# A second half of the feed-forward layer in a seven-product form, with weight sums made by accumulating DMAs

## The chip, the cores and the metric

The kernel runs on one core of one Trainium2 chip. The metric is the device time of one execution in microseconds (us); lower is better. The core has a matrix engine (PE, with weight loads listed as PEld), a vector engine (DVE), a scalar engine (ACT), GpSimd (POOL), and a synchronisation engine (SP) that issues most of the DMAs. PE adds its sums into PSUM; the other operands stand in SBUF, and the large arrays in DRAM.

## The reference

The reference is a decoder trunk of two layers on 1024 tokens of width 1024, in float32. Each layer has a mixer and then a feed-forward part, which is what the change touches:

```python
for layer in range(DEPTH):                       # DEPTH = 2
    ...
    x = x + y                                    # y: the mixer's output
    h = rmsnorm(x, ffn_norm_g[layer])
    x = x + jnp.square(jax.nn.relu(h @ ffn_w1[layer])) @ ffn_w2[layer]
return rmsnorm(x, final_norm_g)
```

`ffn_w1` is 1024 x 4096 and `ffn_w2` is 4096 x 1024. The product with `ffn_w2` is called the output product below, the one with `ffn_w1` the input product.

## The kernel before

All arrays are held transposed: features on the 128 partitions, the 1024 tokens along the free axis, so a tile of 128 x 1024 float32 (512 KB) is one block of features. `X` is eight such tiles. Every dense product is made in three terms. An operand is split into a high part (ACT casts it, line 99) and a low remainder (DVE subtracts, line 100), and a block of 128 x 128 weights meets a slice of activations in three matmuls: high by high, high by low, low by high (lines 149 to 151). In the names, `wr` is a weight tile as loaded, `wh` and `wl` are its parts; `ft` is a loaded tile of the hidden layer, `fh` and `fl` are its parts. There are 3 buffers for `wr` and 8 for `wh` and `wl` together, that is four weight tiles; the 128 x 1024 tiles of all other kinds (`ft`, `fh`, `fl`, `x`, `hid` and more) come from one pool of 34 slots.

`ffn` (line 430) does the feed-forward part. It first calls `ffn_in` (line 298), which makes the input product already in a seven-product form: each of 16 units makes two feature blocks of the hidden layer in seven products of a quarter of the size (names B11, B21, T2, T1, T3, B22, T4), with the sums `T2`, `T1`, ... of the activations and the sums `S1`, `S2`, ... of the weights made on DVE. The unit takes relu and square on ACT and stores the two tiles `hid` to DRAM by DMAs that ACT issues (lines 408 and 411).

The output product then goes in eight chunks over K (4096). `hload(c)` loads the four hidden tiles of a chunk, DVE multiplies each by `acc`, which by then holds the squared scale of the norm (line 443), and they are split. `out_chunk` (line 269) loads the weights of the chunk in four tiles, and for each of them makes two output blocks in two halves of 512 tokens: 12 matmuls (4 hidden tiles by three terms) into a PSUM tile `mm`, which DVE adds into `X` (line 293). In the last chunk the tokens go in four segments of 256 (`SEGS`), so that the norm of the next layer (`norm_sq`, `norm_fin`) can be made segment by segment beside it; after layer 1 that is the final norm, and `norm_fin` stores to the output.

A scheduler places the instructions of each engine in an order; each engine, SP too, then runs its own list in order, and an instruction that waits holds up all that stand behind it on the same engine. `high_priority(HP)` moves splits and evictions ahead in that order. DMAs issued by SP and ACT go through two queues (q1 and q10 of the page).

Of the kernel before, what the change touches and what calls it, by code (L numbers as in the profile page):

```python
# [35 lines left out]
def hs(half):  # L36
    return slice(half * HALF, (half + 1) * HALF)
# [7 lines left out]
def R(ap):  # L45
    return ap.bitcast(F32R)
# [10 lines left out]
class Trunk:  # L57
# [131 lines left out]

    def norm_start(self, X, g, split=True):  # L190
        lo = [self.slot("hl") for _ in range(NT)]
        hi = [self.slot("hh") for _ in range(NT)] if split else None
        return dict(X=X, g=g, acc=None, lo=lo, hi=hi, split=split)

    def norm_sq(self, st, i, r):
        nc = self.nc
        if st["acc"] is None:
            st["acc"] = self.slot("acc")
        if i == 0:
            nc.scalar.activation(st["acc"][:, r], st["X"][0][:, r], AF.Square)  # L200
        else:
            t = self.small([P, r.stop - r.start], "sq")
            self.sq = nc.scalar.activation(t, st["X"][i][:, r], AF.Square)
            nc.vector.tensor_tensor(st["acc"][:, r], st["acc"][:, r], t, ALU.add)

    def norm_fin(self, st, r, ps=None):
        nc, split = self.nc, st["split"]
        n = r.stop - r.start
        if ps is None:
            ps = self.psum_parts(st["acc"], r)  # L210
# [68 lines left out]
    def out_chunk(self, wsrc, acts, X, norm=None, fill=0, segs=(hs(0), hs(1))):  # L279
# [26 lines left out]
        else:  # L306
            ws = [[self.wload(src[ob]) for src in wsrc] for ob in range(4)]
            for j, r in enumerate(segs):
                for ob in (0, 2, 1, 3):
# [4 lines left out]
                    if not wino and j > 0 and ob == 2:  # L314
                        self.norm_fin(norm, segs[j - 1])


    def ffn_in(self, l, st, hid, load):

        nc, ops, tt = self.nc, st["ops"], self.nc.vector.tensor_tensor  # L320
# [61 lines left out]
        def square(t, src=None):  # L382
            self.last_relu = nc.scalar.activation(t, t if src is None else src, AF.Relu)
            nc.scalar.activation(t, t, AF.Square)

        def unit(u, ws):
# [24 lines left out]
            nc.scalar.dma_start(hid[2 * u + 1], h1)  # L411

# [17 lines left out]
    def ffn(self, l, st, xd, norm_g):  # L430
        nc = self.nc
        hid = self.dp.tile([FF // P, P, T], F32, name=self.nm("hid"))
        w2 = self.a["w2"][l]
        X = [self.slot("x") for _ in range(NT)]
        norm = norm_g(X)

        def hload(c):
            hs_ = []
            for k in range(4 * c, 4 * c + 4):
                t, hh, hl = self.slot("ft"), self.slot("fh"), self.slot("fl")  # L440
                nc.sync.dma_start(t, hid[k])
                with self.tc.high_priority(HP):
                    nc.vector.tensor_tensor(t, t, st["acc"], ALU.mult)
                    self.last_split = self.split(t, hh, hl)
                hs_.append((hh, hl))
            return hs_

        cur = self.ffn_in(l, st, hid, hload)
        with self.tc.issue_after(self.last_split.ins):
            for o in range(NT):  # L450
                nc.sync.dma_start(X[o], xd[o])
# [4 lines left out]
        return X, norm  # L456

# [416 lines left out]
    def conf_half(self, i, ws, half, acts, fill=0, nlow=0, fin=None):  # L874
# [5 lines left out]
        if fin is not None:  # L880
            self.norm_fin(fin, SEGS[-1])
        pg = self.mm_ps()
# [218 lines left out]
    def odd(self, st, norm_g):  # L1101
# [9 lines left out]
        prs = [self.conf_pair(i) for i in range(2)]  # L1111
        self.conf_half(0, prs[0], 0, acts, fin=st)
        self.conf_half(1, prs[1], 0, acts)
        for i in range(2):
            self.conf_half(i, prs[i], 1, acts)
            self.conv31(i, prs[i][2])
# [58 lines left out]
    def build(self):  # L1175
        tc, nc, a = self.tc, self.nc, self.a
        with tc.tile_pool(name="kp", bufs=1) as self.kp, tc.tile_pool(name="wp", bufs=1) as self.wp, \
# [18 lines left out]

            st = self.norm_start(X, "mixg0")
            self.gmlp(st)
            X, norm = self.ssd(st, lambda X: self.wino_start(X, "ffng0", self.xd[0]))
# [10 lines left out]
            X, norm = self.ffn(1, norm, self.xd[2], lambda X: self.norm_start(X, "fing", False))  # L1210
            self.norm_fin(norm, SEGS[-1])

def layout(inputs):
# [52 lines left out]
    r["w1"] = np.stack([blocks(f("ffn_w1")[l]) for l in range(2)])  # L1268
    r["w2"] = np.stack([kout(f("ffn_w2")[l], 4, 256) for l in range(2)])
    return r  # L1270
# [20 lines left out]
```

## Time and profile before

| | |
|---|---|
| time, median of 3 runs | 2853.62 us (2852.7 to 2854.3) |
| profiled execution: its own time | 2856.86 us |
| profiled execution: span, first to last instruction | 2855.1 us |
| PE busy | 2815.4 us (99%) |
| DVE / ACT / POOL busy | 1927.6 (68%) / 1198.3 (42%) / 4.0 us |
| DMA traffic | 287.23 MB, mean 101 GB/s |

The profile is of one execution, so its parts add up to its own time of 2856.86 us, which is 3.2 us above the median. A busy share is of the whole span; a wait that matters shows as a hole in PE's row.

### The profile page before, as it was taken

How to read it: one execution, taken by the hardware profiler on the slowest of the kernel's cores; microseconds unless marked ns; L12 is line 12 of the kernel's file. 1: busy time of each engine (PE TensorE's matmuls, PEld its weight loads, DVE VectorE, ACT ScalarE, POOL GpSimd, SP SyncE). 2: the span in 40 equal slices, each digit the busy share in tenths (PEclk: the TensorE clock that was granted, in tenths of full speed). 3: DMA queues.
4: the chain of work that ended last, by engine and by line, in shares of the span. 5: the costliest groups of instructions: out<-in, count | busy, mean ns of one | idle time of the engine just before them, and what ended most of it. 6: DMA issues, size and time to landing. Idle time of an engine off the chain costs nothing.

```text
span 2855.1 us, 36628 instructions
## 1 busy us (share of the span) xinstructions
PE 2815.4 (99%) x14637; PEld 2361.8 (83%) x14637; DVE 1927.6 (68%) x2985; ACT 1198.3 (42%) x1964; POOL 4.0 (0%) x16
## 2 busy tenths in 40 slices
PE   8999998999999999999999999998999999999998
PEld 8988786778788888889888888888888888888887
DVE  5666878768544566546699998885769544566546
ACT  6421425226655532113534444455347655522112
POOL 0000000000000000000000000000000000000000
PEclk9999999999999999999999999999999999999999
DMA  4131424513333453221211111113313332543211
GB/s 163 45 98 64 140 66 149 188 52 111 118 118 102 150 191 128 86 74 46 102 52 60 63 57 53 53 59 126 139 52 104 133 105 102 175 180 118 85 56 60
DMA packets 100027, 287.23 MB, mean 101 GB/s; under 512 B 10768, under 2 KB 33680, under 8 KB 99856
## 3 DMA queue, kind: packets, MB, share of 16 engines
q1 hardware_dynamic: 83440, 242.47, 26.0%
q10 hardware_dynamic: 16416, 42.42, 3.8%
q8 instruction: 115, 1.88, 0.3%
q14 instruction: 56, 0.46, 0.1%
HBM read 217.61 MB, written 67.24 MB: 100 GB/s over the span
## 4 chain that ended last, share of the span: by engine, by line
PE 93%; DVE 5%; ACT 1%; DMA 1%; issue 1%; SPq 0%; DVEq 0%
PE mm L149 19%; PE mm L151 19%; PE mm L150 19%; PE mm L330 6%; PE mm L331 6%; PE mm L332 6%; PE mm L160 3%; PE mm L161 3%; PE mm L162 3%; DVE cy L900 2%; PE sm L331 1%; PE sm L330 1%; PE sm L332 1%; PE sm L724 1%; PE sm L186 1%
## 5 line engine op out<-in xcount | busy, mean ns | idle before, releaser
L293 DVE TENSOR_TENSOR x<-x,mm 128x512 f32<-128x512 f32 (+1 forms) x416 | 258.8, 623 | 295.3 <-PE mm L151 282.3
L99 ACT CAST wh<-wr 128x1024 fp32r<-128x1024 f32 (+1 forms) x180 | 188.6, 1048 | 567.2 <-PE mm L150 502.3
L149 PE MATMUL mm<-fh,wh 128*128 128x512 f32 (+1 forms) x1152 | 424.9, 369 | 0.0
L151 PE MATMUL mm<-fh,wl 128*128 128x512 f32 (+1 forms) x1152 | 423.6, 368 | 0.0
L150 PE MATMUL mm<-fl,wh 128*128 128x512 f32 (+1 forms) x1152 | 422.4, 367 | 0.0
L149 PE MATMUL mm<-hh,wh 128*128 128x512 f32 x960 | 384.5, 400 | 0.0
L151 PE MATMUL mm<-hh,wl 128*128 128x512 f32 x960 | 379.3, 395 | 0.0
L150 PE MATMUL mm<-hl,wh 128*128 128x512 f32 x960 | 378.5, 394 | 0.0
L900 DVE SCALAR_TENSOR_TENSOR cy<-ag,vec,cy 128x1023 f32<-128x1023 f32 (+14 forms) x240 | 303.8, 1266 | 3.8
L100 DVE TENSOR_TENSOR wl<-wr,wh 128x1024 fp32r<-128x1024 f32 (+1 forms) x180 | 219.9, 1223 | 75.4 <-ACT wh L99 75.1
L151 PEld LDWEIGHTS mm<-fh,wl 128*128 128x128 f32 x1152 | 216.6, 188 | 38.5
L150 PEld LDWEIGHTS mm<-fl,wh 128*128 128x128 f32 x1152 | 216.5, 188 | 38.2
L149 PEld LDWEIGHTS mm<-fh,wh 128*128 128x128 f32 x1152 | 216.9, 188 | 36.9
L160 PE MATMUL mm<-wh,hh 128*128 128x256 f32 (+1 forms) x768 | 219.7, 287 | 9.6 <-ACT hh L225 8.7
L161 PE MATMUL mm<-wl,hh 128*128 128x256 f32 (+1 forms) x768 | 217.4, 284 | 0.8 <-DVE wl L100 0.8
L162 PE MATMUL mm<-wh,hl 128*128 128x256 f32 (+1 forms) x768 | 216.7, 283 | 0.0
L149 PEld LDWEIGHTS mm<-hh,wh 128*128 128x128 f32 x960 | 181.4, 189 | 42.4 <-issue 2.8
L150 PEld LDWEIGHTS mm<-hl,wh 128*128 128x128 f32 x960 | 180.9, 188 | 41.2 <-issue 1.8
L151 PEld LDWEIGHTS mm<-hh,wl 128*128 128x128 f32 x960 | 180.7, 188 | 41.4
L330 PE MATMUL mm<-T,wq 128*128 128x512 f32 x512 | 201.1, 394 | 0.6 <-ACT snap L379 0.6
L331 PE MATMUL mm<-T,wq 128*128 128x512 f32 x512 | 201.2, 394 | 0.0
L332 PE MATMUL mm<-T,wq 128*128 128x512 f32 x512 | 200.6, 394 | 0.0
(299 smaller groups left out, 5055.7 us busy)
## 6 DMA issues: line engine op xcount, KB each, us to landing
wr<-in_w_dram SPq DMA_DIRECT2D x134, 512.0 KB, 3.7
hid<-hid ACTq DMA_DIRECT2D x64, 512.0 KB, 3.6
ft<-hid SPq DMA_DIRECT2D x64, 512.0 KB, 4.8
x<-xd SPq DMA_DIRECT2D x24, 512.0 KB, 10.8
A<-acs_d SPq DMA_DIRECT2D x16, 512.0 KB, 5.9
wr<-in_wig_dram SPq DMA_DIRECT2D x16, 512.0 KB, 3.6
wr<-in_wxbc_dram SPq DMA_DIRECT2D x12, 512.0 KB, 3.6
wr<-in_wv_dram SPq DMA_DIRECT2D x8, 520.0 KB, 6.0
```

What stands on the lines that cost most here:

```text
L100: return self.nc.vector.tensor_tensor(R(lo), t, h, ALU.subtract)
L149: mm(ps, R(wh[:, c]), R(ah[:, r]), start=(first and k == 0), stop=False)
L150: mm(ps, R(wh[:, c]), R(al[:, r]), start=False, stop=False)
L151: mm(ps, R(wl[:, c]), R(ah[:, r]), start=False, stop=(last and k == n - 1))
L160: mm(ps[:, :n], R(ah[:, r]), R(wh[:, c]), start=(k == 0), stop=False)
L161: mm(ps[:, :n], R(ah[:, r]), R(wl[:, c]), start=False, stop=False)
L162: mm(ps[:, :n], R(al[:, r]), R(wh[:, c]), start=False, stop=(k == len(acts) - 1))
L293: nc.vector.tensor_tensor(X[o][:, r], X[o][:, r], ps, ALU.add)
L330: mm(ps, R(w[:, c]), R(b[:, L]), start=(first and k == 0), stop=False, skip_group_check=not first)
L331: mm(ps, R(w[:, c]), R(b[:, H]), start=False, stop=False, skip_group_check=not first)
L332: mm(ps, R(w[:, cl]), R(b[:, L]), start=False, stop=(last and k == 3), skip_group_check=not first)
L900: nc.vector.scalar_tensor_tensor(d, st[:, :T - k], w, d, ALU.mult, ALU.add)
```

## The change

The output product is made in a seven-product form too. With the tokens in two halves and the outputs and K in two halves, seven products of half of K (16 blocks), half of the outputs (4 blocks, `o`) and half of the tokens (512) give all four quarters of the result:

- The seven activation operands B11, B21, N2, N1, T3, B22 and N4 are made in `ffn_in`, on DVE, from the unit's results. Each is an array of its own in DRAM; ACT stores three of them and SP four (256 KB per unit and operand, in place of two stores of 512 KB by ACT).
- The weight operands are `w2` in four quarters (`w2` is laid out by `quads` on the host) and four sums of quarters, `ws[0]` to `ws[3]`. `combine` makes the sums in DRAM: POOL first copies a column of `acc` (`gate`), then issues 64 DMAs of 512 KB per layer, DRAM to DRAM, of which 32 copy and 32 add to what stands at the destination.
- The products go one after another over all of their K. For each, `hload` loads eight tiles (`m`) and, for each `o`, `wload` loads two (`c`). The eight PSUM tiles (`pa[o]`, `pc[o]`) keep sums over products; where a product completes a partial sum of a quarter, ACT copies it to `X` or DVE adds it. The multiplication by `acc` is done on the result (`fin`), no more on the loaded hidden tiles; `fin` also loads the residual `xr` in 256 KB pieces in place of `X` in eight tiles.
- The next norm is made in halves of 512 (second half H first, then first half L); at the end of the kernel L goes in two segments of 256.

Per layer, the counts are: matmuls of 512 columns 1344 before and now; matmuls of 256 columns 384 before, none now; hidden tiles loaded and split 32 before, 56 now; weight tiles loaded and split 32 before, 56 now.

```diff
@@ ffn_in: unit
             s1 = snap(pa)
             tt(h0[:, L], s1, pb, ALU.add)
             square(h0[:, L])
+            put("B11", u, h0[:, L])
...
             square(h1[:, H])
+            put("B22", u, h1[:, H])
             prod(pc, ws(), "B22", False, True)
             tt(h0[:, H], s2, pc, ALU.add)
             square(h0[:, H])
-            nc.scalar.dma_start(hid[2 * u], h0)
+            h2 = self.slot("hid")
+            tt(h2[:, H], h0[:, L], h0[:, H], ALU.subtract)
+            put("N1", u, h2[:, H], nc.sync)
+            neg_sub(h2[:, L], h2[:, H], h1[:, H])
+            put("N2", u, h2[:, L], nc.sync)
+            tt(h0[:, H], h1[:, H], h0[:, H], ALU.subtract)
+            put("T3", u, h0[:, H], nc.sync)
             prod(pa, ws(), "T4", False, True)
             square(h1[:, L], pa)
-            nc.scalar.dma_start(hid[2 * u + 1], h1)
+            put("B21", u, h1[:, L])
+            neg_sub(h2[:, L], h2[:, L], h1[:, L])
+            put("N4", u, h2[:, L], nc.sync)
@@ new
+    def combine(self, w, after):
+        n = w.shape[0]
+        s = [self.dp.tile([n, P, T], F32, name=self.nm("ws")) for _ in range(4)]
+        a11, a12, a21, a22 = (w[:, i] for i in range(4))
+        add = dict(accum_op=ALU.add)
+        for dst, src, kw in ((s[0], a21, {}), (s[1], a11, {}), (s[2], a11, {}), (s[3], a12, {}), (s[0], a22, add),
+                             (s[1], s[0], add), (s[3], s[1], add), (s[2], a21, add)):
+            for u in range(n):
+                with self.tc.issue_after(after.ins):
+                    self.nc.gpsimd.dma_start(dst[u], src[u], max_dma_last_dim=4096, **kw)
+        return s
@@ ffn
-        for c in range(NT):
-            nxt = hload(c + 1) if c < NT - 1 else None
-            self.out_chunk([w2[c]], [cur], X, norm=norm if c == NT - 1 else None, segs=SEGS)
-            cur = nxt
...
+        plan = (("B11", w2[:, 0]), ("B21", w2[:, 1]), ("N2", ws[1]), ("N1", ws[0]), ("T3", ws[2]), ("B22", ws[3]),
+                ("N4", w2[:, 3]))
+        for n, (name, wsrc) in enumerate(plan):
+            for m in range(NT):
+                if (name, m) not in ready:
+                    hload(name, m)
...
+            for o in range(4):
+                w = [self.wload(wsrc[2 * o + c]) for c in range(2)]
+                if n == 0:
+                    pa[o] = self.mm_ps()
+                elif n in (1, 3):
+                    pc[o] = self.sm_ps()
+                ps = pc[o] if n in (1, 3, 5) else pa[o]
+                prod(ps, w, name, n in (0, 1, 3))
+                if n == 0:
+                    copy(X[o][:, L], ps)
+                elif n == 1:
+                    add(X[o][:, L], ps)
+                    fin(o, L, None, 1)
...
+                else:
+                    fin(o + 4, L, ps, -1)
+                if n == 6 and o == 0:
+                    self.norm_fin(box["norm"], H)
```

In this text the products are n0 to n6 in the order of `plan`. SP's list shows how the loads of one product follow those of another. The first piece is of the kernel before, at the middle of layer 0's output product: `ft` are the hidden tiles of the coming chunk, `wr` the weights.

```order
L107 DMA wr1310_8700<-in_w2_dram 128x1024
L441 DMA ft1240_8217<-hid823_5742 128x1024
L107 DMA wr1329_8790<-in_w2_dram 128x1024
L441 DMA ft1243_8224<-hid823_5742 128x1024
L441 DMA ft1246_8231<-hid823_5742 128x1024
L107 DMA wr1336_8852<-in_w2_dram 128x1024
L441 DMA ft1277_8486<-hid823_5742 128x1024
L107 DMA wr1343_8914<-in_w2_dram 128x1024
```

The second is of the changed kernel, also on SP in layer 0, at the step from n0 to n1: `wr1324` is the weight tile of n1's o1 (second half), `wr1330` and `wr1333` those of o2, `wr1339` and `wr1342` those of o3, `ft1288` to `ft1303` the first six of n1's eight hidden tiles, and `wr1372` the first tile of n2's weights, the sum `ws[1]`.

```order
L107 DMA wr1324_8812<-in_w2_dram 128x1024
L107 DMA wr1330_8875<-in_w2_dram 128x1024
L107 DMA wr1333_8881<-in_w2_dram 128x1024
L485 DMA ft1288_8690<-hid824_5743 128x1024
L107 DMA wr1339_8944<-in_w2_dram 128x1024
L485 DMA ft1291_8696<-hid824_5743 128x1024
L485 DMA ft1294_8702<-hid824_5743 128x1024
L485 DMA ft1297_8708<-hid824_5743 128x1024
L485 DMA ft1300_8714<-hid824_5743 128x1024
L485 DMA ft1303_8720<-hid824_5743 128x1024
L107 DMA wr1342_8950<-in_w2_dram 128x1024
L107 DMA wr1372_9061<-ws832_5752 128x1024
```

Before, hidden tiles and weights alternate one by one. Now all weight tiles of n1 up to `wr1339`, the seventh of eight, and only one hidden tile stand ahead of the second hidden tile; the last two hidden tiles of n1 come behind `wr1372`. `wr1339` waits for the buffer of `wr1324`, so for the split of n1's fourth weight tile (o1, second half); `wr1372` waits for the accumulating DMA that makes its source.

ACT's list at the same place, in the changed kernel (`x1243` is the last of the four sums of n0 that ACT copies to `X`; `wh1325` is the weight tile of n1's o1, second half):

```order
L99 CAST wh1325_8814<-wr1324_8812 128x1024
L527 COPY x1243_8413<-mm1287_8640 128x512
L99 CAST fh1289_8691<-ft1288_8690 128x1024
L99 CAST fh1292_8697<-ft1291_8696 128x1024
L99 CAST fh1295_8703<-ft1294_8702 128x1024
L99 CAST fh1298_8709<-ft1297_8708 128x1024
L99 CAST wh1331_8877<-wr1330_8875 128x1024
L99 CAST fh1301_8715<-ft1300_8714 128x1024
```

`wh1325` waits for the buffer of a weight tile of n0's last group, which PE must have finished; `x1243` waits for PE's last matmul of n0; the first hidden tile of n1 comes behind both.

Before, ACT's casts of hidden tiles (`fh`) stood between those of the weights, each a chunk ahead of its use. Now the first cast for a product comes behind work that waits for the end of the product before. PE's list at the start of n1 takes the hidden tiles one by one, each for the 6 matmuls of o0 and the 6 of o1 (the tile's two blocks by three terms), before it goes on to the next tile; the step from n3 to n4 has the same order on all three engines. POOL's list holds the gate and the 64 DMAs of a layer, and a DMA waits for the one that stands eight places ahead of it.

## Rows read from the trace of the kernel before

**Rows 1.** The page: busy time, and the engines' shares of the chain that ended last.

```profile
PE 2815.4 (99%) x14637; PEld 2361.8 (83%) x14637; DVE 1927.6 (68%) x2985; ACT 1198.3 (42%) x1964; POOL 4.0 (0%) x16
...
PE 93%; DVE 5%; ACT 1%; DMA 1%; issue 1%; SPq 0%; DVEq 0%
```

**Rows 2.** Windows: input product, then output product (512, then 256 columns), both layers.

```profile
core 0: us, PE busy (x) PEld busy (x) DVE busy (x) ACT busy (x) POOL busy (x), PEclk, DMA share, GB/s
...
705.00:1002.00 297.00, 296.69 (x1279) 239.38 (x1278) 155.05 (x259) 180.22 (x326) 1.06 (x2) 1.00 0.35 118
1002.00:1312.00 310.00, 310.00 (x1348) 252.91 (x1347) 177.91 (x210) 62.45 (x67) 0.00 (x0) 1.00 0.33 113
1312.00:1358.00 46.00, 45.99 (x386) 45.67 (x385) 37.77 (x92) 21.67 (x51) 0.00 (x0) 1.00 0.19 65
...
2190.00:2487.00 297.00, 296.75 (x1281) 240.19 (x1281) 155.79 (x262) 181.12 (x328) 0.00 (x0) 1.00 0.35 119
2487.00:2796.00 309.00, 309.00 (x1348) 252.78 (x1347) 175.77 (x199) 62.12 (x64) 0.00 (x0) 1.00 0.32 110
2796.00:2842.00 46.00, 46.00 (x389) 45.84 (x388) 35.40 (x90) 17.24 (x41) 0.00 (x0) 1.00 0.15 49
```

**Rows 3.** Groups by line and shape, 1002 to 1358.6 us: xcount, busy us, mean ns, idle.

```profile
L293 DVE TENSOR_TENSOR x<-x,mm 128x512 f32<-128x512 f32 x112 | 76.8, 686 | 106.5 <-PE mm L151 103.3 <-DMA x<-xd 3.0
L100 DVE TENSOR_TENSOR wl<-wr,wh 128x1024 fp32r<-128x1024 f32 x32 | 39.1, 1223 | 3.5 <-ACT wh L99 3.3
...
L443 DVE TENSOR_TENSOR ft<-ft,acc 128x1024 f32<-128x1024 f32 x28 | 34.2, 1221 | 11.7 <-DMA ft<-hid 11.7
L99 ACT CAST wh<-wr 128x1024 fp32r<-128x1024 f32 x31 | 32.5, 1050 | 133.8 <-PE mm L150 133.8
L99 ACT CAST fh<-ft 128x1024 fp32r<-128x1024 f32 x28 | 29.4, 1051 | 110.2 <-DVE ft L443 80.1 <-PE mm L150 23.8 <-DMA ft<-hid 6.3
```

**Rows 4.** A group of 705 to 1002 us: ACT's copies from PSUM.

```profile
L379 ACT COPY snap<-mm 128x512 f32<-128x512 f32 x61 | 35.5, 586 | 72.8 <-PE mm L332 69.5 <-DVE ws L345 3.3
```

**Rows 5.** The page: DMA issues, KB each, median us from issue to landing.

```profile
wr<-in_w_dram SPq DMA_DIRECT2D x134, 512.0 KB, 3.7
...
ft<-hid SPq DMA_DIRECT2D x64, 512.0 KB, 4.8
x<-xd SPq DMA_DIRECT2D x24, 512.0 KB, 10.8
```

**Rows 6.** Window of 3 us in which loads are queued: clock, DMA share, GB/s.

```profile
1015.00:1018.00 3.00, 1.00 1.04 418
```

**Rows 7.** Timeline of SP, 1000 to 1020 us: start, us for the row.

```profile
1004.41 0.33 SPq L107 DMA_DIRECT2D wr<-in_w_dram  x1
...
1015.47 0.32 SPq L441 DMA_DIRECT2D ft<-hid  x1
```

**Rows 8.** Waits, 1002 to 1358 us: total, times, longest.

```profile
SPq L107 <- DVE wl L100: 234.6, 27, 11.0
...
ACT wh L99 <- PE mm L150: 133.8, 27, 10.1
```

**Rows 9.** Windows of PE around a fall of the clock: us, busy, clock, DMA, GB/s.

```profile
1754.50:1757.90 3.40, 1.89 (x10) 1.00 0.73 205
1757.90:1761.30 3.40, 3.40 (x10) 0.50 0.25 104
```

**Rows 10.** Timeline of PE at the same place.

```profile
1757.91 0.60 PE L150 MATMUL mm<-hl,wh 128*128 128x512 f32 x1
...
1761.30 0.41 PE L149 MATMUL mm<-hh,wh 128*128 128x512 f32 x1
```

**Rows 11.** Timeline of the end of the program.

```profile
2842.22 0.28 PE L151 MATMUL mm<-fh,wl 128*128 128x256 f32 x1
...
2844.55 0.70 PE L186 MATMUL sm<-acc,cm 128*128 128x256 f32 x2 [2.06 <-DVE acc L204]
...
2848.34 3.26 DVE L217 SCALAR_TENSOR_TENSOR hl<-x,vec,rs 128x256 f32<-128x256 f32 x8
```

More of the change, by code (lines that the diff above doesn't have):

```diff
@@ L190, in norm_start, with norm_out @@
     def norm_start(self, X, g, split=True):
-        lo = [self.slot("hl") for _ in range(NT)]
-        hi = [self.slot("hh") for _ in range(NT)] if split else None
-        return dict(X=X, g=g, acc=None, lo=lo, hi=hi, split=split)
+        return dict(X=X, g=g, acc=None, lo=[None] * NT, hi=[None] * NT, split=split)
+    def norm_out(self, st):
+        for i in range(NT):
+            if st["lo"][i] is None:
+                st["lo"][i] = self.slot("hl")
+                if st["split"]:
+                    st["hi"][i] = self.slot("hh")
     def norm_sq(self, st, i, r):
@@ L198, in norm_sq @@
             st["acc"] = self.slot("acc")
-        if i == 0:
-            nc.scalar.activation(st["acc"][:, r], st["X"][0][:, r], AF.Square)
+        if r.start not in st.setdefault("begun", set()):
+            st["begun"].add(r.start)
+            nc.scalar.activation(st["acc"][:, r], st["X"][i][:, r], AF.Square)
         else:
@@ L430, in ffn @@
     def ffn(self, l, st, xd, norm_g):
-        nc = self.nc
-        hid = self.dp.tile([FF // P, P, T], F32, name=self.nm("hid"))
+        nc, tt = self.nc, self.nc.vector.tensor_tensor
         w2 = self.a["w2"][l]
-        X = [self.slot("x") for _ in range(NT)]
[L435 to L451, printed above, removed]
-        for c in range(NT):
-            nxt = hload(c + 1) if c < NT - 1 else None
-            self.out_chunk([w2[c]], [cur], X, norm=norm if c == NT - 1 else None, segs=SEGS)
-            cur = nxt
-        return X, norm
+        L, H = hs(0), hs(1)
+        hid = {n: self.dp.tile([NT, P, T], F32, name=self.nm("hid")) for n in ("B11", "B21", "N2", "N1", "T3", "B22", "N4")}
@@ new lines, in ffn, with hload, early @@
+        ws = self.combine(w2, self.gate(st["acc"]))
+        ready = {}
+        def hload(name, m):
+            t, hh, hl = self.slot("ft"), self.slot("fh"), self.slot("fl")
+            nc.sync.dma_start(t, hid[name][m])
+            with self.tc.high_priority(HP):
+                self.split(t, hh, hl)
+            ready[name, m] = hh, hl
+        def early(_):
+            for m in range(4):
+                hload("B11", m)
+        self.ffn_in(l, st, hid, early)
+        rs = st["acc"]
+        X = [self.slot("x") for _ in range(NT)]
@@ new lines, in ffn, with prod @@
+        box = {}
+        def prod(ps, w, name, first):
+            mm = nc.tensor.matmul
+            for c in range(2):
+                wh, wl = w[c]
+                for k in range(8):
+                    m, j = (c * 8 + k) // 2, k % 2
+                    hh, hl = ready[name, m]
+                    r, cw = hs(j), slice(k * P, k * P + P)
+                    st_, sp_ = first and c == 0 and k == 0, c == 1 and k == 7
+                    mm(ps, R(wh[:, cw]), R(hh[:, r]), start=st_, stop=False, skip_group_check=not first)
+                    mm(ps, R(wh[:, cw]), R(hl[:, r]), start=False, stop=False, skip_group_check=not first)
+                    mm(ps, R(wl[:, cw]), R(hh[:, r]), start=False, stop=sp_, skip_group_check=not first)
@@ new lines, in fin, with copy @@
+        def fin(i, r, ps, sign, last=False):
+            x = X[i][:, r]
+            t = self.small([P, HALF], "xr")
+            nc.sync.dma_start(t, xd[i][:, r])
+            with self.tc.high_priority(HP):
+                if ps is not None:
+                    tt(x, ps, rs[:, r], ALU.mult)
+                else:
+                    tt(x, x, rs[:, r], ALU.mult)
+                tt(x, t, x, ALU.add if sign > 0 else ALU.subtract)
+                self.norm_sq(box["norm"], i, r)
+        def copy(x, ps):
+            with self.tc.high_priority(HP):
+                nc.scalar.copy(x, ps)
@@ new lines, in add @@
+        def add(x, ps):
+            with self.tc.high_priority(HP):
+                tt(x, x, ps, ALU.add)
+        pa, pc = [None] * 4, [None] * 4
+        plan = (("B11", w2[:, 0]), ("B21", w2[:, 1]), ("N2", ws[1]), ("N1", ws[0]), ("T3", ws[2]), ("B22", ws[3]),
[4 more added lines that the diff above has]
+                    hload(name, m)
+            if n == 1:
+                box["norm"] = norm_g(X)
+            for o in range(4):
[11 more added lines that the diff above has]
+                    fin(o, L, None, 1)
+                elif n == 2:
+                    copy(X[o][:, H], ps)
+                elif n == 3:
+                    copy(X[o + 4][:, H], ps)
+                elif n == 4:
+                    add(X[o + 4][:, H], ps)
+                    fin(o + 4, H, None, -1)
+                elif n == 5:
+                    add(X[o][:, H], ps)
+                    fin(o, H, None, 1)
+                else:
+                    fin(o + 4, L, ps, -1)
+                if n == 6 and o == 0:
+                    self.norm_fin(box["norm"], H)
+            for m in range(NT):
+                del ready[name, m]
```

26 lines of the change are left out of this document (20 added, 6 removed).

## The prediction

> **What bounds the kernel now.** I read the page first, then the windows by stage, then the groups, waits and timeline of the stage that changes. PE is busy 99% of the span and holds 93% of the chain that ended last [rows 1], so no other engine limits the kernel: time can go only with PE's work, and any hole in PE's work is new time. By stages [rows 2], the output product of layer 0 is 310 us of matmuls of 512 columns and then 46 us of 256 columns, layer 1 the same, and PE is busy in all of it; DVE is busy 57% of it (177.91 of 310), ACT 20%, the DMA engines a third. In the input product (297 us a layer) DVE is at 52%, ACT at 61%, DMA at 0.35. The waits of this stage [rows 8] are those of engines that are ahead: SP waits 234.6 us in all, up to 11 us a time, for a split that frees a weight buffer, and ACT waits up to 10.1 us for PE to free `wh`. Weights are thus loaded as early as four of them fit, no earlier; hidden tiles are a chunk ahead. That lead is what the change rearranges.
>
> **The gain.** Matmuls of 512 columns: 310.00 us for 1348 is 0.230 us each, and their number stays (1344 a layer). The 384 of 256 columns go: 46.0 us for 386 to 389 is 0.119 each [rows 2], so 384 x 0.119 = 45.7 us a layer, **91.5 us** in both.
>
> **Work on other engines.** The multiplications by `acc` go (32 x 1.22 us of DVE [rows 3]); 24 more hidden and 24 more weight tiles come, each 1.05 us of ACT and 1.22 us of DVE. DVE's additions into `X` shrink from 112 of 0.686 us to 12 additions from PSUM and the 512-wide `fin` operations. DVE then has 112 x 1.22 + (12 + 16 x 3) x 0.686 = 178 us (three operations for each of 16 `fin`), ACT 112 x 1.05 + 12 x 0.586 [rows 4] + 16 squares at the same = 134 us, over 310: neither becomes the bound, if spread evenly. In the input product four 512-wide DVE operations a unit come, 16 x 4 x 0.686 = 44 us, so DVE goes from 52% to 67%. They hang on results already off PE, so I cost them at nothing; what hides them is the slack of DVE, and when they run late the third hidden slot of the unit and the stores in SP's list run late, then the weights of the next unit behind those stores. For this, and for the larger traffic there, I put 1.5 us a layer (0 to 10: a full input-product unit is 297/16 = 18.6 us, so half a unit at most).
>
> **The steps from product to product.** Here the hidden tiles are no longer a chunk ahead. Take the step n0 to n1 with PE's end of n0 at time 0. ACT must cast `wh1325` (1.05, its buffer is freed by PE's last matmuls), copy the last sum (0.59), then cast the first hidden tile (1.05); with hops PE starts near 3.0, and its second matmul, on the low part (1.22 on DVE), at 4.1. I take 3.5. Meanwhile SP waits for DVE's split of the same `wr1324` (done at 2.4), issues `wr1339`, and only then the hidden tiles m1 to m5, at some 0.33 us an issue [rows 7]. A load alone lands 3.7 us after issue [rows 5], and queued loads follow at 524 KB / 418 GB/s = 1.25 us [rows 6]: `wr1339` lands near 6.2, m1 at 7.5, m2 at 8.7, m3 at 10. PE has 12 matmuls (2.8 us) for each tile: m0 lasts from 3.5 to 6.3; m1 is cast at 8.6 and lasts to 11.4; m2 to 14.2; m3 to 17.0; then o2 waits about 0.6 for its weights. That is 17.6 us for 48 matmuls that need 11.1: **6.5 to 7 us** of holes. n3 to n4 has the same order. The other steps are milder: within n0 the fourth weight group waits for PE's end of the third (2 us); n1 to n2 has m2 and m3 late (2 us), the three others 0.5 each. Per layer 2 x 7 + 2 + 2 + 1.5 = 19.5.
>
> The clock adds to it. After a stretch in which PE was busy 1.89 of 3.40 us, the granted clock was 0.50 in the next 3.40 us, that is the lower level of 1.2 GHz [rows 9]; there eight matmuls came in 3.39 us, 0.424 each in place of 0.230 [rows 10], so 1.6 us lost. The big steps have such a stretch (PE busy 2.8 of the 8.6 us from 0), perhaps for longer, so I add 2 us to each: 4 a layer. The Trainium skill, page "TensorE: Matmul & The Clock Gate", section "Why this matters for your kernels", warns against idle gaps between bursts of matmuls, since a long enough one sets the clock back to half; the trace agrees that the clock falls behind a thinly filled stretch, but there were several short gaps in it. By the page it is the single gap that counts: should the longest here, 3.5 us, not do, the 8 us for the clock would go and the sum would be 2811.
>
> Together 23.5 a layer, **47 us**. The lower bound is 0 for steps where the loads come earlier than I place them; the upper one: x<-xd loads of a full queue land 10.8 us after issue [rows 5], 7 us later than I take. With 7 us more on both big steps of a layer it is 28 us more, 75.
>
> **The weight sums.** No DRAM-to-DRAM DMA, none that accumulates and none that POOL issues stands in the trace. They start with `gate`, when the norm's `acc` is complete (near 705), and the first tile of `ws[1]`, the 41st of 64, is wanted by SP about 5 us into n1, at 1002 + 44.2 + 5 = 1051 (192 matmuls x 0.230 = 44.2 a product). From below: 1.25 us each by the bytes [rows 6]. From above: 10.8 us [rows 5] and one after the other. With eight in flight I take 2 x 1.25 = 2.5 for a copy and 3 x 1.25 = 3.8 for an addition (each byte is read, or read twice, and written): 32 x 2.5 + 32 x 3.8 = 200 us, beside the 0.35 of DMA that the input product takes and some 0.12 for the new stores. 705 + 200/0.53 = 1082 for all 64; the 41st (32 x 2.5 + 9 x 3.8 = 114 us of engine time) is done at 705 + 114/0.53 = 920, 131 us ahead. So it costs nothing on PE's path; what covers it is the input product. If it is late, SP stands at `wr1372` and with it the last two hidden tiles of n1.
>
> **The ends.** After layer 0 the next mixer begins with the half that is normed first, behind it the L half has some 16 us of matmuls as cover: 0. After layer 1: before, the last matmul starts at 2842.22, the norm's matmul at 2844.55, the eight last scalings from 2848.34 for 3.26 us, and the span ends at 2855.1 [rows 11]. Now the chain ahead of the norm's matmul has four 512-wide operations in place of three of 256 (2.9 for 2.0 us), two rstd chains run into each other (1), and 16 scalings follow in place of 8 (+3.3), with eight more stores of some 0.35 us behind: **6.5 us** (5 to 8).
>
> **Sum.** 2856.9 (the profiled execution's own time) - 91.5 + 47 + 3 + 6.5 = 2821.9. The median of the runs is 3.2 us below the profiled execution: **2819**.
>
> **Rivals.** *A, as worked out*, holes of 35 to 60 us: 2805 to 2832. Chance 0.47. *B, the holes are larger*: the queue at the steps behaves as the x loads do, or POOL's transfers run into the loads of n0 to n3; 28 us more give 2847, so 2832 to 2848; 0.17. The Trainium skill, page "DMA: Bandwidth & Descriptors", section "Issuing engines are not separate DMA queues", says that transfers issued by SP, ACT and POOL share the same engines and interleave; it speaks for B as long as the sums are in flight after 1002, and no run here shows POOL's. *C, the holes stay away*: SP's DMA waits are often short of what I assumed and PE's order lets o0 run on. Before, PE's holes in this stage are next to nothing (310.00 busy of 310 [rows 2]), which speaks for it; against it, that hidden tiles then stood a chunk ahead. 0 to 35 us of holes: 2772 to 2805; 0.22. *D, the sums come too late*, which ends above: the limit for the 41st is (1051 - 705)/41 = 8.4 us a DMA. At 10.8 each, one after another, it is ready at 705 + 443 = 1148, 97 us late, in each layer: 2819 + 194 = 3013. At 9 us a DMA it would be 23 us late, twice: 2865. For it speaks that DRAM to DRAM and the addition are unknown; against it, that eight are in flight and the x loads' 10.8 is a latency in a full queue whose loads end 1.25 apart. 0.10. Between B and D, 0.04 lies within 0.2% of before (5.7 us, about what a measurement of this kernel can tell from no change). *The change does not do what it says* is excluded: the counts of matmuls are in the program.
>
> **How the numbers follow.** The likeliest is A, 2819; its own range 2805 to 2832. The 80% range leaves out C's lower end and D: 2778 to 2850. Faster by over 0.2%: A, B and C less B's edge, 0.84; the same 0.05; slower 0.11, D and the end of B.
>
> **What the next profile would show.** PE's records of 512 columns at 0.230 us and none of 256 in the output product; holes of 3 to 4 us at the start of n1 and n4, and one of some 2 us before m1, released by ACT's cast of `fh`, itself by DMA `ft`; a clock of 0.50 behind them; output products of 332 us a layer and a tail of 19. SP's wait at the first `ws[1]` load would be short of POOL's DMAs. Wrong would be the prediction if that wait is tens of us (D), or if PE's busy share in n0 to n6 is above 98% (C).

## The result, and the profile after

| | before | changed |
|---|---|---|
| time, median | 2853.96 us (4 runs) | 2966.94 us (2966.25 to 2967.37, 4 runs) |
| ratio to before | | 1.0395 (95% interval 1.0377 to 1.0413) |
| span of the profiled execution | 2855.1 us | 2964.8 us |

The changed kernel is 4% slower; 2819 us and a gain of 1.2% were predicted. The page of the changed kernel, beside [rows 1], [rows 5]:

```profile
span 2964.8 us, 35789 instructions
PE 2788.9 (94%) x13863; PEld 2292.4 (77%) x13863; DVE 1921.8 (65%) x2865; ACT 1286.0 (43%) x2024; POOL 90.0 (3%) x146
...
PE   8999998996789998999999999999996799989997
...
DMA  4132425319964465455211111114239954464544
...
q0 software_dynamic: 18432, 67.12, 9.3%
...
PE 74%; DMA 11%; DVE 9%; ACT 3%; issue 2%; SPq 0%; ACTq 0%; DVEq 0%
...
ws<-in_w_dram POOLq DMA_DIRECT2D x96, 512.0 KB, 12.4
...
ws<-ws POOLq DMA_DIRECT2D x32, 512.0 KB, 10.3
```

PE is at 94%, no more at 99%, and a tenth of the chain is DMA. In the rows of slices (each digit is the busy share of a fortieth of the span, in tenths) PE's sixes and sevens stand in the slices of DMA's nines, once in each layer; the last seven is the end of the program. That is where POOL's queue (q0, new) makes the sums of weights. The same stages as in [rows 2], with the odd mixer and the ends, as windows of the changed kernel (even output product, input product, output product, odd mixer, odd output product, input product, output product, end):

```profile
481.00:702.00 221.00, 205.67 (x1044) 167.99 (x1043) 146.13 (x264) 70.81 (x107) 11.44 (x23) 0.96 0.46 149
702.00:1071.00 369.00, 330.08 (x1350) 262.40 (x1350) 204.29 (x354) 190.25 (x354) 31.56 (x43) 0.94 0.69 204
1071.00:1412.60 341.60, 322.99 (x1348) 253.68 (x1347) 182.78 (x203) 135.86 (x159) 1.05 (x2) 0.98 0.56 191
1412.60:2030.00 617.40, 609.32 (x3798) 532.08 (x3797) 527.02 (x622) 275.16 (x452) 1.64 (x8) 0.99 0.18 60
2030.00:2238.80 208.80, 200.27 (x1030) 166.56 (x1030) 141.59 (x245) 96.93 (x164) 10.82 (x22) 0.98 0.42 144
2238.80:2607.70 368.90, 329.70 (x1350) 261.72 (x1349) 205.53 (x357) 191.50 (x357) 32.13 (x44) 0.94 0.69 207
2607.70:2946.30 338.60, 321.80 (x1348) 251.60 (x1346) 173.31 (x181) 127.40 (x144) 0.00 (x0) 0.98 0.52 182
2946.30:2964.80 18.50, 1.26 (x5) 0.68 (x4) 11.36 (x27) 3.01 (x7) 0.00 (x0) 0.64 0.32 113
```

The same windows of the kernel before are 205.8, 313.2, 356.6, 617.4, 198.5, 312.8, 355.2 and 12.6 us, and its first begins 2 us later. Two of them, the input and the output product of layer 0:

```profile
688.80:1002.00 313.20, 312.89 (x1350) 252.63 (x1349) 170.88 (x298) 192.04 (x353) 1.06 (x2) 1.00 0.35 120
1002.00:1358.60 356.60, 356.59 (x1735) 299.18 (x1734) 216.28 (x304) 84.72 (x119) 0.00 (x0) 1.00 0.31 107
```

So the difference of 109.7 us is +15.2, +55.8, **-15.0**, 0, +10.3, +56.1, **-16.6**, +5.9 and -2. The output product, which the change is about, did become shorter. The 137 us are lost ahead of it, in the input product (the same 1344 matmuls as before) and in the mixer's output product before that, which the change does not touch at all. Part of the loss there is a granted clock of 0.94: PE is busy 330 us for matmuls that took 313.

What held PE up where the sums are made, by the waits of 690 to 860 us (total, times, longest):

```profile
DVE hid L417 <- DMA hid<-hid: 34.7, 4, 12.0
...
PE mm L357 <- ACT snap L406: 23.9, 5, 8.0
ACT x L262 <- DMA xd<-x: 22.7, 7, 6.3
ACT wq L99 <- DVE ws L372: 17.3, 4, 11.0
```

PE waits for ACT's copy from PSUM, ACT stands behind work that waits for a DMA, itself or through DVE. The longest row is not a wait for a free slot. Line 417 (`neg_sub`) makes N2 in one half of `h2`, and later N4 in the same half; N4 may not be written before the store of N2 has landed, and DVE's whole list waits with it. In DVE's timeline the first row makes N2 and the second N4:

```profile
809.56 0.69 DVE L417 SCALAR_TENSOR_TENSOR hid<-hid,hid 128x512 f32<-128x512 f32 x1
...
822.87 0.69 DVE L417 SCALAR_TENSOR_TENSOR hid<-hid,hid 128x512 f32<-128x512 f32 x1 [12.02 <-DMA hid<-hid]
```

In the same way ACT may not scale `x` in place (line 262) before its spill to `xd` has landed, and a new `hid` tile may not be begun before the stores of an older one have freed its slot. In the kernel before no wait for a DMA stands among the seven longest rows of this stretch. One link of the chain of waits, 768 to 785 us, is such a slot (start, us):

```profile
767.42 14.16 DMA hid<-hid
...
781.69 0.61 ACT hid L410
...
783.46 0.47 ACT snap L406
```

A store of 256 KB landed 14.16 us after issue. The DMA table of 668 to 842 us, in which the sums are made, shows that the other transfers are late too: first the queues (packets, MB, share of the 16 DMA engines), then the issues (x, KB, median us to landing):

```profile
q0 software_dynamic: 9216, 33.56, 78.6%
q1 hardware_dynamic: 3838, 10.08, 16.0%
q10 hardware_dynamic: 4032, 5.24, 9.2%
...
wr<-in_w_dram SPq DMA_DIRECT2D x12, 512.0 KB, 9.8
hid<-hid SPq DMA_DIRECT2D x15, 256.0 KB, 10.2
hid<-hid ACTq DMA_DIRECT2D x12, 256.0 KB, 8.2
xd<-x ACTq DMA_DIRECT2D x15, 128.0 KB, 10.5
```

The sums do begin at 668 us and not at 705: `gate` reads column 0 of `acc`, which is complete with the first 512 tokens. The first was issued at 668.1, the last at 831.7 and landed at 841.7, 304 us ahead of SP's first load of a sum (1145.4). Nothing waited for a sum.

POOL's list lets a transfer go when the one eight places ahead has landed. By the landing times in the trace fewer were in flight: at most seven of the copies, and three of the additions once they follow one another (the eighth addition was issued at 749.99 us, when the fifth had landed at 749.68 and the sixth and seventh had not). What sets this limit is not shown. Where this text says eight in flight, it means that no other limit was put on POOL.

### The profile page after: what moved, and what is told of

The parts are those of the page before. It is cut to its first block, busy times and chain, and to the rows that moved or that the text cites. A ratio compares the mean times of both kernels' runs of the same rounds, so it can differ in the third digit from the quotient of the medians.

```text
span 2964.8 us, 35789 instructions
## 1 busy us (share of the span) xinstructions
PE 2788.9 (94%) x13863; PEld 2292.4 (77%) x13863; DVE 1921.8 (65%) x2865; ACT 1286.0 (43%) x2024; POOL 90.0 (3%) x146
## 4 chain that ended last, share of the span: by engine, by line
PE 74%; DMA 11%; DVE 9%; ACT 3%; issue 2%; SPq 0%; ACTq 0%; DVEq 0%
PE mm L149 10%; PE mm L150 10%; PE mm L151 10%; PE mm L358 4%; PE mm L357 4%; PE mm L359 4%; DMA hid<-hid 3%; DMA xd<-x 3%; DMA ft<-hid 3%; PE mm L509 3%; PE mm L508 3%; PE mm L160 3%; PE mm L510 3%; PE mm L161 3%; PE sm L509 2%; PE sm L508 2%
## 5 line engine op out<-in xcount | busy, mean ns | idle before, releaser
L99 ACT CAST wh<-wr 128x1024 fp32r<-128x1024 f32 (+1 forms) x228 | 238.4, 1047 | 520.1 <-PE mm L150 244.6
L100 DVE TENSOR_TENSOR wl<-wr,wh 128x1024 fp32r<-128x1024 f32 (+1 forms) x228 | 278.5, 1224 | 256.5 <-ACT wh L99 211.8
L357 PE MATMUL mm<-T,wq 128*128 128x512 f32 x512 | 213.8, 418 | 60.1 <-ACT snap L406 39.4
L358 PE MATMUL mm<-T,wq 128*128 128x512 f32 x512 | 212.2, 415 | 12.6 <-DVE T L100 12.4
L100 DVE TENSOR_TENSOR fl<-ft,fh 128x1024 fp32r<-128x1024 f32 x112 | 136.5, 1223 | 124.9 <-ACT fh L99 124.6
L359 PE MATMUL mm<-T,wq 128*128 128x512 f32 x512 | 209.8, 410 | 0.2 <-DVE wq L100 0.2
L508 PE MATMUL mm<-fh,wh 128*128 128x512 f32 x512 | 194.8, 400 | 16.0 <-ACT fh L99 14.2
L509 PE MATMUL mm<-fl,wh 128*128 128x512 f32 x512 | 203.3, 401 | 2.4 <-DVE fl L100 2.4
L510 PE MATMUL mm<-fh,wl 128*128 128x512 f32 x512 | 202.2, 398 | 1.1 <-DVE wl L100 1.1
L99 ACT CAST fh<-ft 128x1024 fp32r<-128x1024 f32 x112 | 117.0, 1048 | 171.0 <-DMA ft<-hid 170.6
L357 PEld LDWEIGHTS mm<-T,wq 128*128 128x128 f32 x512 | 102.4, 200 | 91.1 <-ACT snap L406 42.4
L508 PE MATMUL sm<-fh,wh 128*128 128x512 f32 x384 | 146.5, 401 | 15.5 <-ACT fh L99 15.5
## 6 DMA issues: line engine op xcount, KB each, us to landing
ws<-in_w_dram POOLq DMA_DIRECT2D x96, 512.0 KB, 12.4
ws<-ws POOLq DMA_DIRECT2D x32, 512.0 KB, 10.3
```

The lines of the kernel that those rows point to most:

```text
L99: self.nc.scalar.copy(R(h), t)
L100: return self.nc.vector.tensor_tensor(R(lo), t, h, ALU.subtract)
L357: mm(ps, R(w[:, c]), R(b[:, L]), start=(first and k == 0), stop=False, skip_group_check=not first)
L358: mm(ps, R(w[:, c]), R(b[:, H]), start=False, stop=False, skip_group_check=not first)
L359: mm(ps, R(w[:, cl]), R(b[:, L]), start=False, stop=(last and k == 3), skip_group_check=not first)
L508: mm(ps, R(wh[:, cw]), R(hh[:, r]), start=st_, stop=False, skip_group_check=not first)
```

## The experiments

**What the sums cost, and what the rest does.** All sums are left out, and the products n2 to n5 load quarters of `w2` in their place:

```diff
-        ws = self.combine(w2, self.gate(st["acc"]))
+        ws = [w2[:, 2], w2[:, 0], w2[:, 0], w2[:, 1]]
```

> The sums of weights are left out: POOL issues no DMA, and n2 to n5 take quarters of w2 in place of ws[0] to ws[3] (so the result is not the reference's). Theory S (POOL's 64 DMAs a layer fill the DMA engines from 668 us on, and the stores of hid and xd and the loads of w1 beside them land 8 to 16 us late, which stops PE): the end of the even output product and the input product go back to about 206 and 315 us a layer, from 221 and 369, the odd output product to 199 from 209, and the time to 2967 - 14 - 54 - 10 - 54 = about 2835 us. Rival R (the input product's own seven stores a unit and four DVE operations a unit are what is too much): the input product stays above 350 us a layer and the time above 2920.

Measured: 2829.32 us, ratio 0.9918 (0.9902 to 0.9935). Its windows for the first input product and for the output products of both layers:

```profile
688.00:1001.40 313.40, 313.16 (x1350) 252.91 (x1349) 203.03 (x352) 189.03 (x351) 0.00 (x0) 1.00 0.47 159
1001.40:1344.00 342.60, 322.99 (x1348) 253.02 (x1348) 182.83 (x203) 136.52 (x159) 1.06 (x2) 0.98 0.55 191
...
2471.20:2809.60 338.40, 321.00 (x1348) 250.95 (x1346) 173.28 (x181) 128.16 (x144) 0.00 (x0) 0.99 0.52 182
```

The input product is back at 313.4 us with PE full, with all seven stores a unit and the four added DVE operations in it. Rival R falls; the sums cost 2964.8 - 2827.9 = 137 us. The DMA table of this run over the same 668 to 842 us:

```profile
q1 hardware_dynamic: 6768, 17.30, 31.1%
q10 hardware_dynamic: 5472, 7.87, 12.5%
...
hid<-hid SPq DMA_DIRECT2D x28, 256.0 KB, 2.1
hid<-hid ACTq DMA_DIRECT2D x22, 256.0 KB, 2.3
```

Stores of 256 KB landed 2.1 to 2.3 us after issue, and the queues of SP and ACT had 43.6% of the engines; beside the sums they had 25.2%.

**The same sums elsewhere.** In the second run POOL makes the sums of both layers in the first input projection; in the third a result of the fifth unit of the input product gates them; in the fourth they go five at a time, one group behind each unit.

```diff
 # early
                 self.rows = st["acc"]
+                go = self.gate(st["acc"])
+                self.ws = [self.combine(a["w2"][l], go) for l in range(2)]
 ...
 # late
+            if u == 4:
+                self.ws = self.combine(self.a["w2"][l], self.gate(self.last_sq))
 # paced, at the end of unit u
+        s, g = self.ws, self.gate(self.last_sq)
...
+        for d, c, kw in todo[5 * u:5 * u + 5]:
+            with self.tc.issue_after(g.ins):
+                self.nc.gpsimd.dma_start(d, c, max_dma_last_dim=4096, **kw)
```

> The same 128 DMAs of POOL as in the changed kernel, but all issued from about 80 us on, in the first input projection, where the DMA share was 0.32 and weights are loaded ahead; nothing else is changed. Theory S: if that stage has slack, the time is that without the sums, about 2835 us, up to 2860 if the projection waits for its loads; the sums end before 500 us. Rival R: above 2920, as without the sums. A third, that such DMAs take the same from PE wherever they run: about 2967.

> The gate of the sums is a result of the fifth unit of the input product (about 790 us) in place of the first half of the norm's sum (668). Theory S, holes wherever the sums meet the stores of hid: the 14 us in the even and 10 in the odd output product and the 16 at the start of the input product go, but some 35 us a layer stay in the later units: about 2900. Rival T (only the start of the input product is sensitive, because its operands wait for the spill to xd): about 2840. The sums then end near 970, ahead of their use at about 1050.

> The sums are issued five DMAs after each unit of the input product, each group gated by the unit's last square, and ws[1] is made first; so at most five are in flight and the rest of the time the DMA engines serve the stores and loads alone. Theory S with a queue that is too deep: the stores land 3 to 8 us after issue, and the time is 2840 to 2870. Rival, that the sum of the traffic is too much for the DMA engines in this stage (share above 0.9): 2900 or more.

Measured: early 2890.78 us, ratio 1.0139 (1.0120 to 1.0157); late 2889.47, 1.0129 (1.0114 to 1.0144); paced 2866.22, 1.0048 (1.0033 to 1.0063). So the paced run lies in theory S's range, the late one near its 2900, and rival T (about 2840) falls. In the late run the even and odd output products recover, as expected, and the holes move into the later units: its first input product is the window of 339.8 us below, 26.4 more than without sums.

```profile
688.40:1028.20 339.80, 320.74 (x1350) 0.98 0.81 245
```

In that input product one long wait for a DMA is left. The first row is of the late run (its line 418 is line 417 of the changed kernel), the second of the run without sums, both of 690 to 1000 us:

```profile
DVE hid L418 <- DMA hid<-hid: 95.4, 12, 12.1
```

```profile
DVE hid L417 <- DMA hid<-hid: 7.7, 12, 1.5
```

It is N4 waiting for the store of N2, once a unit; the next wait for a DMA in the late run's list is 1.9 us. The paced run has the same row with 90.1 us. So where the sums meet only the later units, this one write in place is what waits for a landing. No run gives N4 a place of its own, so how much of the loss that alone would take away is not shown.

The early run did not come near 2835 and is above the 2860 allowed for it: the first projection had no slack for eight transfers in flight either. Its window of 70 to 480 us has a DMA share of 0.87, and PE is 41 us short (4 us without sums):

```profile
70.00:480.00 410.00, 368.81 (x1893) 0.94 0.87 233
```

**How many in flight.** After every DMA of a sum (later: after every second or fourth) POOL loads 32 bytes of its result and copies a column of that, and the next waits for the copy:

```diff
                 with self.tc.issue_after(after.ins):
                     self.nc.gpsimd.dma_start(dst[u], src[u], max_dma_last_dim=4096, **kw)
+                for _ in range(1):
+                    t = self.kp.tile([1, 8], F32, tag="tick", bufs=1, name=self.nm("tick"))
+                    self.nc.gpsimd.dma_start(t, dst[u][0:1, 0:8])
+                    after = self.gate(t)
```

In the early runs of this kind layer 1's sums follow layer 0's.

> The sums start at the same gate (668 us) and are the same 64 DMAs a layer, but one at a time: after each, POOL loads 32 bytes of the result, copies a column of it, and only then issues the next. Theory Q (it is the depth of eight that hurts: stores and loads stand behind up to 4 MB of POOL's transfers): stores land at most 3 to 4 us later than without the sums, and the time is 2830 to 2850. Rival V (the volume hurts: each sum takes its engine time from stores and loads wherever it falls): like five at a time, 2866, or more. If a sum takes over 8 us in this way, ws[1] is late and n2 starts with a hole, which would show on SP.

> The sums of both layers one at a time, layer 0's from about 80 us on, layer 1's behind them. At some 6 us a sum they end near 850 us, ahead of every use. Theory Q: 2829 to 2840 us, as without the sums, and with the right result, so faster than before by 0.5 to 0.9%. Rival V: the 57 us that 128 sums took in the first stage with eight in flight stay, about 2885.

Measured: one in flight from the old gate 2963.62 us, 1.0389 (1.0359 to 1.0419); early and one in flight 2854.44, 1.0001 (0.9983 to 1.0019). Both miss theory Q's times (2830 to 2850, and 2829 to 2840). The windows of the first tell two things apart (input product, then output product, layer 0):

```profile
684.30:1000.00 315.70, 313.84 (x1350) 1.00 0.67 213
...
1000.20:1407.50 407.30, 331.97 (x1347) 0.90 0.66 197
```

The input product with sums beside it all the time takes 315.7 us, 2.3 more than without: theory Q holds there, though only 35 of the layer's 64 sums, most of them copies, were issued in that time. A sum now takes some 9.5 us (64 issued from 665 to 1270 us), and the output product waits for the sums themselves, as SP's waits of 1002 to 1407 us show:

```profile
SPq L107 <- DMA ws<-in_w_dram: 96.7, 8, 33.9
```

This is the prediction's rival D, made by hand; that the time is near the changed kernel's is chance. In the early run one at a time, the last sum was issued at 1234 us, so layer 1's sums ran beside layer 0's output product, whose window grew to 361.9 us from 342.6 without sums.

> As the early sums one at a time, but two in flight. One at a time took 9 us a sum, ended at 1242 us and reached into layer 0's output product, whose holes grew by 20 us. At two in flight a pair should take some 10 to 11 us, 64 pairs end near 760, ahead of the input product's end. Theory Q (depth hurts, and else only sums that run beside a sensitive stage): 2830 to 2838 us. Rival V (volume hurts): 2850 or more, since all 128 now fall before 1002.

> As the early sums, four in flight: between two and eight (2891). They end near 500 us. Theory Q: the first stage grows by 10 to 30 us, in all 2842 to 2862. Rival V: the same as with two.

Measured: two in flight 2855.09 us, 1.0006 (0.9995 to 1.0016); four 2866.61, 1.0056 (1.0036 to 1.0076). Both expectations of Q were too low. Rival V's time for two in flight (2850 or more) came out, but not its other claim, that four are the same as two: the two intervals stand apart. (Of the additions no more than three were in flight with four allowed.) With two in flight the sums ended near 826, and the windows say where they cost:

```profile
60.00:290.00 230.00, 230.00 (x1258) 197.98 (x1258) 145.82 (x250) 75.82 (x105) 48.61 (x87) 1.00 0.58 175
...
487.00:704.50 217.50, 203.75 (x1041) 166.09 (x1042) 143.10 (x255) 70.66 (x107) 40.13 (x75) 0.98 0.70 202
704.50:826.00 121.50, 114.13 (x476) 89.45 (x475) 88.40 (x175) 78.68 (x160) 20.23 (x33) 0.99 0.81 215
826.00:1027.80 201.80, 201.80 (x875) 164.51 (x875) 116.31 (x182) 112.34 (x195) 0.17 (x1) 1.00 0.47 163
```

In the projection up to 290 us PE is full beside the sums; in the even output product and in the input product it is not, and as soon as the sums end it is full again. Depth is thus only a part of it: the stage is another.

**The stage.** Layer 0's sums stay early, two in flight; layer 1's go beside the odd mixer, two or eight in flight. Both runs also have the hidden tiles of n1 to n6 loaded by POOL (below), and the small memsets of POOL in the odd mixer made by DVE.

```diff
+                self.ws = [self.combine(a["w2"][0], self.gate(st["acc"]))]
...
             X, norm = self.ffn(0, norm, self.xd[0], lambda X: self.norm_start(X, "mixg1"))
...
+            self.ws.append(self.combine(a["w2"][1], self.gate(norm["acc"])))
```

> As the run with early sums two at a time and hidden tiles by POOL, but layer 1's sums start at the end of layer 0's output product (near 1350 us) and run beside the odd projection, whose DMA share was 0.18; nothing of them is left beside the even output product and the input product (which stood at 20 us more than without sums). The small memsets of POOL in the odd stage go to DVE, so that they don't stand behind the sums. Theory Q: 2837 - 20 = about 2817 us, at most 5 above it. Rival: the odd stage is as easily disturbed as the first one, 2825 to 2840.

> As the run before it, with eight of layer 1's sums in flight in the odd stage instead of two. If what decides is how far ahead a stage loads, and the odd stage's small traffic leaves its loads well ahead: the same to 5 us more. If eight in flight stop PE wherever a load is waited for: 20 to 28 us more, half of what 128 sums took in the first stage.

Measured: two 2813.29 us, 0.9861 (0.9838 to 0.9883); eight 2811.43, 0.9857 (0.9839 to 0.9875). The first is 4 us better than theory Q's 2817, the second as the first of its two cases expected. With eight, the sums were issued from 1336 to 1483 us; the window of that time, and one row of its DMA table:

```profile
1331.00:1500.00 169.00, 169.00 (x982) 146.26 (x981) 140.22 (x157) 70.57 (x107) 43.33 (x65) 1.00 0.99 262
...
wr<-in_wig_dram SPq DMA_DIRECT2D x6, 512.0 KB, 7.8
```

The DMA engines are at 0.99 and PE is busy for all of the 169 us. Weight loads land 6.9 to 8.5 us after issue there (medians by the DMA table of that stretch), and no engine's list of waits has one for a load there. In the input product the same depth and the same lateness stopped PE. So full DMA engines, or POOL issuing, cost no time by themselves; what costs it is a stage in which work waits for a landing soon after issue.

**The steps from product to product.** Without sums, all hidden tiles are loaded by POOL; then, with the early sums two in flight, all but those of n0:

```diff
-            nc.sync.dma_start(t, hid[name][m])
+            nc.gpsimd.dma_start(t, hid[name][m])
 # then
+            (nc.sync if name == "B11" else nc.gpsimd).dma_start(t, hid[name][m])
```

> As the run without sums (they are left out again), and the hidden tiles ft are loaded by POOL, not SP, so that they no longer stand behind the weight loads in SP's list. Theory of the prediction (the holes at n0 to n1 and n3 to n4 come from that order): of the 29 to 33 us of holes a layer, 11 and 8 at these two steps, 5 to 7 go at each, and the time falls by 20 to 28 us to about 2805. Rival (the holes come from PE's order, in which the slots for the next tiles come free only in the last group of a product, and from ACT's casts): less than 8 us, 2822 or more.

> As the run before it, and the hidden tiles of n1 to n6 (not of n0) are loaded by POOL. In the run where all were, holes at n1 fell from 11.3 to 6.6 us and at n4 from 8.7 and 7.5 to 6.1, but n0's grew from 4 to 10. If n0's come from POOL's loads of n0 alone, this gives some 9 us a layer: 2812 to 2822. If POOL's loads only move the holes from one product to the next, nothing: 2830 to 2838.

Measured: 2822.26 us, 0.9889 (0.9874 to 0.9904), so 7 us less than without sums (the two intervals overlap at their edges), where the theory said 20 to 28 and its rival less than 8; and 2837.53, 0.9941 (0.9926 to 0.9955), 17.6 less than the run with early sums and SP's loads (not the 2812 to 2822 that were expected, since that run itself had come out 20 us above its expectation). The hole at the start of n1 of the changed kernel, and of the run with all hidden tiles by POOL (timeline of PE, two kernels):

```profile
1128.61 1.22 PE L508 MATMUL sm<-fh,wh 128*128 128x512 f32 x2 [7.05 <-ACT fh L99]
```

```profile
1027.97 0.80 PE L509 MATMUL mm<-fl,wh 128*128 128x512 f32 x1 [4.67 <-DVE fl L100]
...
1058.50 0.73 PE L508 MATMUL sm<-fh,wh 128*128 128x512 f32 x2 [2.84 <-ACT fh L99]
```

The one hole of 7.05 us became one of 2.84, but the one within n0 grew to 4.67 us, from 2.16 in the run without sums. With n0's tiles by SP again, and the sums out of the way, the output products are 330.0 and 332.1 us (run with two in flight beside the odd mixer):

```profile
999.50:1329.50 330.00, 317.76 (x1348) 251.99 (x1347) 181.50 (x203) 133.69 (x158) 24.87 (x47) 0.99 0.57 198
...
2457.70:2789.80 332.10, 320.44 (x1348) 253.17 (x1346) 172.04 (x181) 125.58 (x143) 24.87 (x47) 0.99 0.53 186
```

That is 12.6 and 6.3 us less than in the run without sums. 21 to 23 us of holes a layer stay, beside 309 of matmuls; what ends them was not taken further.

## Why the prediction was wrong

**What failed is the part on the weight sums**: "So it costs nothing on PE's path; what covers it is the input product." The working asked only whether the sums would be ready for their use. They were, earlier than worked out: the last at 842 us, where 1082 was estimated, and the two prices, 2.5 and 3.8 us, were not far off (the 32 copies were there at 733 us, 2.0 each from 668 on, the 32 additions 108 us later, 3.4 each, with the other traffic beside them). The wrong step is the 0.53: it lets the stage's own traffic keep its 0.47 of the DMA engines and gives the sums what is left. In the trace the sums took 0.79 from 668 to 842 us, and the queues of SP and ACT had 0.25, where they have 0.44 without sums. A store of 256 KB that lands 2.1 to 2.3 us after issue without sums landed after 8.2 to 10.2 in the median, and the write of N4 over N2, the slots of `hid`, the in-place scaling of `x` and the loads of `w1` have no such lead. Measured: 137 us in place of 0.

Rival B had the mechanism ("POOL's transfers run into the loads of n0 to n3"), and the Trainium skill's sentence beside it (page "DMA: Bandwidth & Descriptors", section "Issuing engines are not separate DMA queues") was borne out: in the 174 us of the sums the three queues shared the engines, 78.6, 16.0 and 9.2%, and the stores of SP and ACT landed some 6 to 8 us later than without POOL's transfers. But rival B was placed in the output product, where the sums had long ended, and priced at 28 us. In front of it, in the input product, I had looked at DVE and at the stores' number, and at no landing time. Rival D, too late sums, did not occur in the changed kernel; it does when the sums are made one at a time.

**The gate**: 705 us was taken for its start, 668 measured. That is why the mixer's output product lost 15.2 and 10.3 us; with a later gate, or without sums, it did not.

**The gain** held: without holes the 1344 matmuls of 0.230 us are 309.1 us, against 356.6 and 355.2 before, 47 and 46 us a layer; 45.7 was predicted.

**The steps from product to product** held in place: the longest holes of layer 0 are at the starts of n1 (7.05 us) and n4 (2.61 us). In all they are 341.6 - 309.1 = 32.5 and 338.6 - 309.1 = 29.5 us a layer, where 23.5 were predicted. Of this PE stood idle for 18.6 and 16.8 us (window less busy time), where the holes were put at 19.5; the other 13.9 and 12.7 us PE was busy beyond the 309.1, where the clock was put at 4. The granted clock of 0.98 makes some 7 us of that, by an estimate (0.02 of the window); the rest is not resolved. Their cause is only partly the order of SP's list: without it 12.6 and 6.3 us went.

**The input product's own additions**: 3 us for both layers were predicted, 0.2 and 1.6 measured without sums. **The end**: 6.5 predicted, 5.9 measured. So with no cost for the sums the prediction was 2819, and the run without sums gives 2829; the steps and their clock, 15 us over in both layers together, more than make the difference. One slip of the sums changes nothing: with 35 us of holes the time is 2772 + 35 = 2807, not the 2805 that stands between rivals A and C.

## What to carry to other kernels

Work given to the DMA engines "in the shadow" of a stage has two prices: whether it is done in time, and what it does to the landing times of that stage's own stores and loads. Look in the trace for what waits for a landing right after issue (above all tiles overwritten in place after a store, here N4 over N2; slots that a store frees; loads one tile ahead), and put bulk transfers where nothing does: here the same 64 transfers, eight in flight, cost some 68 us a layer beside the input product and its run-up, and nothing that can be seen beside the odd mixer. Where they can't be moved, few in flight help, as long as they still end in time. The version with both, and with the hidden tiles of n1 to n6 loaded by POOL, is 1.4% faster than the kernel before, where the change as made was 4% slower.

## What the runs showed of the hardware

- DRAM-to-DRAM transfers of 512 KB issued by POOL, eight in flight, landed 12.4 us (copies and additions from `w2`, median) and 10.3 us (additions from another sum) after issue. One in flight beside the input product, copies landed 4.6 us after issue; one in flight from 940 to 1280 us, additions from another sum landed after 6.5 us.
- Without a limit of the program below eight, at most seven such copies, and three such additions in steady sequence, were in flight.
- Full DMA engines cost nothing in one stage: a share of 0.99 for 169 us, weight loads at 6.9 to 8.5 us, PE busy throughout.
- Holes cost twice: the clock granted in 690 to 705 us of the changed kernel, where PE was busy for 8.10 of 15 us, was 0.66, and in the whole input product 0.94 (means of stretches at 1.2 and at 2.4 GHz).
